# A zero-padded operand of 128 rows for the second product of the RWKV scan step

## The chip, the cores and the metric

The kernel runs on one core of one Trainium2 chip. The metric is the device time of one execution in microseconds (us), as the median of several runs. The profile shows one execution, taken by the hardware profiler. Its engines are PE (the matrix engine; PEld is its weight load), DVE (VectorE), ACT (ScalarE), POOL (GpSimd) and SP (SyncE, whose queue issues the transfers). L676 is line 676 of the kernel; in the changed kernel the lines behind line 614 stand one to two lines lower (the product of L664 is then at L665; L676 and what follows it keep their numbers).

## The reference

Two layers of a latent diffusion backbone over 1024 latent tokens and 256 context tokens of width 1024, in float32. Each layer projects its normed input into four groups of heads, mixes each group in its own way (2-D neighbourhood attention, multi-head latent attention, RWKV-7 time mixing in both directions, differential attention), joins them in an output projection, and then runs a gated channel mixer. The change lies in the RWKV group, a recurrence with a state of 64x64 per head:

```
def rwkv7_scan(r, decay, k, v, a, b, s0, reverse):
    def step(S, inp):
        r_t, w_t, k_t, v_t, a_t, b_t = inp
        sa = jnp.einsum('bhij,bhj->bhi', S, a_t)
        S = S * w_t[:, :, None, :] + sa[..., None] * b_t[:, :, None, :] + v_t[..., None] * k_t[:, :, None, :]
        return S, jnp.einsum('bhij,bhj->bhi', S, r_t)
    ...
    s_final, y = lax.scan(step, s0, xs, reverse=reverse)
```

There are four heads and two directions.

## The kernel before

The recurrence is done in chunks of 64 tokens. Ahead of the scan, `prep_gen` and `lanes_gen` make for each chunk the small matrices that a step needs and keep them in device memory; the scan loads them as `SG` (slices `ARM`, `RB`, `BT`) and `XB` (the inverse of a triangular 64x64 matrix per head and direction).

`rw_step_gen` is the scan: 20 steps of 64 tokens per layer, 40 in all. A step works on two directions `d`, two head pairs `p` and the two heads `e` of a pair; head `e` sits in rows 64e to 64e+63. All its sums go to one tile of the matrix engine's memory, `pall`. A step is a chain:

1. L664: eight products of 128 rows give `pd`. L667: ACT copies all of `pd` to `Dt`.
2. L676: eight products of `XB` with `Dt`, each on the 64 rows of its head, give `psa`. L678 and L679: ACT copies the half of head 0, and DVE the half of head 1, into `V1`, whose other halves hold the chunk's values. (In the trace `V1` is called V.)
3. L688: eight products of 128 rows with `V1` give `pss`. L696: DVE adds them to the decayed state and writes the next state into `VS`.
4. L706 and L708: sixteen products give the output `py`, which L712 (ACT) copies to `yt`, and L716 stores.

The scan is one of several generators that are advanced in turns: the attention of two groups runs beside it, and the modulation of the next part (`ada_gen`, tiles `adw` and `adaps`), later `rw_out_gen`. `rw_out_gen` turns the scan's outputs into the RWKV part of the mixed rows: a chain of small products (L748, L757, L768, L774, L781) with DVE, ACT and POOL work between them, and at the end the store L784 of `oy` into `ymix`. A unit of it covers 256 tokens of one head pair, and starts when the scan has come far enough. When all groups have stored their part of `ymix`, the output projection loads it (L1775, tiles `h_l`), splits it and multiplies (tiles `pso`, at the helper's lines 140 to 142).

The kernel doesn't write out the order of an engine by hand. A scheduler with a model of its own simulates the program as it is built, and sets each engine's order from that. Each engine then runs its list in order, and so does SP with the transfers: whatever stands behind an instruction that waits, waits too. Where two instructions write one tile, the later one in the program waits for the earlier: L679 waits for L678, although their halves of `V1` are apart.

Of the kernel before, what the change touches and what calls it, by code (L numbers as in the profile page):

```python
# [9 lines left out]
F32 = mybir.dt.float32  # L10
F32R = mybir.dt.float32r
AF = mybir.ActivationFunctionType
# [5 lines left out]
P = 128  # L18
# [22 lines left out]
class K:  # L41
# [561 lines left out]
    def rw_step_gen(self, l, pool, sgp, yp, psp, ptag, need_ctx, F):  # L603
        nc = self.nc
        TT, ACT, MM = nc.vector.tensor_tensor, nc.scalar.activation, nc.tensor.matmul
        segs = ([8, 9] + list(range(8)), [9, 8] + list(range(8))[::-1])
        sg = {}

        def need(i):
            return max(self.SLOT.index(segs[d][i]) for d in range(2))  # L610

        def step_y(i):
            return i >= 2 or need_ctx

        SZ = pool.tile([P, 2, 2, 2, 64], F32, name="SZ", bufs=1)
        for e in range(2):
            nc.gpsimd.memset(SZ[64 - 64 * e:128 - 64 * e, e], 0.0)

        def seg(i):
            SG = sgp.tile([P, 2, 1792], F32, tag="SG", name="SG", bufs=2)  # L620
            XB = pool.tile([P, 2, 4, 64], F32, tag="XB", name="XB", bufs=2)
            VS = pool.tile([P, 2, 2, 2, 2, 64], F32, tag="VS", name="VS", bufs=2)
            W = pool.tile([P, 2, 2, 2], F32, tag="W", name="W", bufs=2)
            for d in range(2):
                sl = self.SLOT.index(segs[d][i])
                vt = self.rvt[sl, d].rearrange("(c s) e p i -> e s c (p i)", c=2)
                for e in range(2):
                    q = slice(64 - 64 * e, 128 - 64 * e)
                    nc.sync.dma_start(VS[q, :, e, d].rearrange("s c p i -> s c (p i)"), vt[e])
                nc.sync.dma_start(SG[:, d], self.rsg[sl, d])  # L630
                nc.sync.dma_start(XB[:, d].rearrange("p u t -> p (u t)"), self.rxf[sl, d].rearrange("p u c t -> p (u c t)"))
                nc.gpsimd.tensor_copy(W[:, :, d], self.Wc[:, sl, d].rearrange("p (a c) -> p c a", a=2))
            if i == 0:
                for e in range(2):
                    nc.gpsimd.memset(VS[64 * e:64 * e + 64, 0, e], 0.0)
            BT = SG[:, :, 0:512].rearrange("p d (e u t) -> p d e u t", e=2, u=4)
            RB = SG[:, :, 512:768].rearrange("p d (u t) -> p d u t", u=4)
            ARM = SG[:, :, 768:1792].rearrange("p d (e u t) -> p d e u t", e=2, u=4)
            sg[i] = (XB, RB, BT, ARM, W, VS)

        while F["lanes"] <= need(0):
            yield
        seg(0)
        for _ in range(3):
            yield
        for step in range(20):
            i, c = step // 2, step % 2
            if c == 1 and i + 1 < 10:
                while F["lanes"] <= need(i + 1):
                    yield  # L650
            if c == 0 and i + 1 < 10 and F["lanes"] > need(i + 1):
                seg(i + 1)
            XB, RB, BT, ARM, W, VS = sg[i]
            V1 = pool.tile([P, 2, 2, 2, 64], F32, tag="V1", name="V1", bufs=2)
            pall = psp.tile([P, 2, 2, 2, 64], F32, tag=ptag, name="pall")
            pd, psa = pall[:, 0], pall[:, 1]
            tmp = pool.tile([P, 2, 2, 64], F32, tag="stmp", name="stmp", bufs=1)
            for e in range(2):
                q = slice(64 - 64 * e, 128 - 64 * e)
                nc.gpsimd.tensor_copy(V1[q, e], VS[q, c, e])  # L660
            for d in range(2):
                for p in range(2):
                    for e in range(2):
                        MM(pd[64 * e:64 * e + 64, d, p], ARM[:, d, e, 2 * p + c, 0:64], VS[:, c, e, d, p], start=True, stop=True)  # L664
            yield  # L665
            Dt = pool.tile([P, 2, 2, 64], F32, tag="Dt", name="Dt", bufs=2)
            ACT(Dt, pd, AF.Copy)  # L667
            for e in range(2):
                r = slice(64 * e, 64 * e + 64)
                nc.gpsimd.tensor_tensor(out=tmp[r], in0=VS[r, c, e], in1=W[r, c, :, :, None].to_broadcast([64, 2, 2, 64]), op=ALU.mult)  # L670
            yield
            for d in range(2):
                for p in range(2):
                    for e in range(2):
                        r = slice(64 * e, 64 * e + 64)
                        MM(psa[r, d, p], XB[r, d, 2 * p + c], Dt[r, d, p], start=True, stop=True)  # L676
            yield
            ACT(V1[0:64, 0], psa[0:64], AF.Copy)  # L678
            nc.vector.tensor_copy(V1[64:128, 1], psa[64:128])  # L679
            if step_y(i):  # L680
                for e in range(2):
                    nc.gpsimd.tensor_copy(SZ[64 * e:64 * e + 64, e], V1[64 * e:64 * e + 64, e])
            yield
            pss, py = pall[:, 0], pall[:, 1]
            for d in range(2):
                for p in range(2):
                    for e in range(2):
                        MM(pss[64 * e:64 * e + 64, d, p], BT[:, d, e, 2 * p + c], V1[:, e, d, p], start=True, stop=True)  # L688
            yield
            if step < 19:  # L690
                if c == 1 and i + 1 not in sg:
                    seg(i + 1)
                nVS = sg[i + c][5]
                for e in range(2):
                    r = slice(64 * e, 64 * e + 64)
                    TT(out=nVS[r, 1 - c, e], in0=tmp[r], in1=pss[r], op=ALU.add)  # L696
            yield
            if not step_y(i):
                yield
                continue  # L700
            for d in range(2):
                for p in range(2):
                    u = 2 * p + c
                    r = [slice(64 * e, 64 * e + 64) for e in range(2)]
                    for e in range(2):
                        MM(py[r[e], d, p], VS[:, c, e, d, p], ARM[:, d, e, u, 64:P], start=True, stop=False)  # L706
                    for e in range(2):
                        MM(py[r[e], d, p], SZ[:, e, d, p], RB[:, d, u], start=False, stop=True)  # L708
            yield
            if c == 0:  # L710
                yt = yp.tile([P, 2, 2, P], F32, tag="yt", name="yt", bufs=2)
            ACT(yt[:, :, :, c * 64:c * 64 + 64], py, AF.Copy)  # L712
            if c == 1:
                for d in range(2):
                    s = segs[d][i]
                    nc.sync.dma_start(self.ryd[d, :, :, s * P:(s + 1) * P], yt[:, d])  # L716
                F["seg"] = i
# [1583 lines left out]
```

## Time and profile before

| | |
|---|---|
| median of 3 runs | 4310.83 us (4297.64 to 4321.85) |
| the profiled execution | 4318.05 us, its span 4316.3 us |
| mean granted clock of the matrix engine | 0.955 of full speed |
| busy share of the span | PE 93%, PEld 77%, DVE 66%, ACT 46%, POOL 19% |
| the two scans | from 627 to 930 us and from 2890 to 3173 us |

The span runs from the first to the last instruction. A busy matrix engine is not one at its peak. The clock is the share of full speed that the throttle granted.

### The profile page before, as it was taken

How to read it: one execution, taken by the hardware profiler on the slowest of the kernel's cores; microseconds unless marked ns; L12 is line 12 of the kernel's file. 1: busy time of each engine (PE TensorE's matmuls, PEld its weight loads, DVE VectorE, ACT ScalarE, POOL GpSimd, SP SyncE). 2: the span in 40 equal slices, each digit the busy share in tenths (PEclk: the TensorE clock that was granted, in tenths of full speed). 3: DMA queues.
4: the chain of work that ended last, by engine and by line, in shares of the span. 5: the costliest groups of instructions: out<-in, count | busy, mean ns of one | idle time of the engine just before them, and what ended most of it. 6: DMA issues, size and time to landing. Idle time of an engine off the chain costs nothing. (4 is left out here: it accounts for less than half of the span.)

```text
span 4316.3 us, 76712 instructions
## 1 busy us (share of the span) xinstructions
PE 4027.8 (93%) x29152; PEld 3319.9 (77%) x29152; DVE 2866.8 (66%) x5946; ACT 1982.7 (46%) x4386; POOL 801.9 (19%) x1320
## 2 busy tenths in 40 slices
PE   6999969999999999899998999969999999999998
PEld 4887856677777778788887887856677777788998
DVE  6577686656676765655556667686776766557666
ACT  4444435535554544433334444435545555435443
POOL 3244122212211112000001344122313111111000
PEclk7999979999999999999999999979999999999999
DMA  6444676655523243221213344687636332333332
GB/s 198 151 134 141 204 226 204 224 160 142 151 82 107 78 149 115 71 64 65 64 59 115 137 135 139 204 233 223 206 98 175 104 106 74 125 104 126 94 98 74
DMA packets 423199, 578.40 MB, mean 134 GB/s; under 512 B 109100, under 2 KB 287660, under 8 KB 421296
## 3 DMA queue, kind: packets, MB, share of 16 engines
q1 hardware_dynamic: 422832, 573.51, 42.9%
q8 instruction: 230, 3.77, 0.4%
q14 instruction: 137, 1.12, 0.1%
HBM read 433.47 MB, written 139.92 MB: 133 GB/s over the span
## 5 line engine op out<-in xcount | busy, mean ns | idle before, releaser
L141 PE MATMUL psm<-h_l,whi 128*128 128x512 f32 (+1 forms) x2112 | 710.3, 336 | 9.2 <-DVE h_l L258 9.0
L140 PE MATMUL psm<-h_h,whi 128*128 128x512 f32 (+1 forms) x2112 | 713.5, 338 | 2.3 <-ACT h_h L257 2.3
L142 PE MATMUL psm<-h_h,wlo 128*128 128x512 f32 (+1 forms) x2112 | 709.0, 336 | 0.0
L1888 DVE SCALAR_TENSOR_TENSOR x<-psm,mod,x 128x258 f32<-128x258 f32 (+2 forms) x616 | 327.0, 555 | 288.3 <-PE psm L142 287.9
L973 ACT ACTIVATE sm_P<-psL,sm_n 128x512 f32<-128x512 f32 (+1 forms) x672 | 392.8, 593 | 266.6 <-DVE sm_n L964 238.5
L141 PEld LDWEIGHTS psm<-h_l,whi 128*128 128x128 f32 x2112 | 399.4, 189 | 54.1 <-DVE h_l L258 12.0
L140 PEld LDWEIGHTS psm<-h_h,whi 128*128 128x128 f32 x2112 | 399.4, 189 | 52.0 <-DVE x L1888 4.0
L142 PEld LDWEIGHTS psm<-h_h,wlo 128*128 128x128 f32 x2112 | 399.1, 189 | 43.4 <-issue 0.2
L962 DVE TENSOR_REDUCE sm_m<-psL 128x1 f32<-128x512 f32 (+1 forms) x640 | 353.0, 578 | 88.0 <-PE psL L803 43.3
L140 PE MATMUL psm<-gh,dhi 128*128 128x510 f32 (+3 forms) x1056 | 364.8, 347 | 10.1 <-ACT mb L1852 5.1
L133 ACT ACTIVATE whi<-wst 128x1024 fp32r<-128x1024 f32 x176 | 186.6, 1060 | 401.2 <-PE psm L141 376.7
L141 PE MATMUL psm<-gl,dhi 128*128 128x510 f32 (+3 forms) x1056 | 357.7, 339 | 0.1
L142 PE MATMUL psm<-gh,dlo 128*128 128x510 f32 (+3 forms) x1056 | 357.4, 339 | 0.0
L134 DVE TENSOR_TENSOR wlo<-wst,whi 128x1024 fp32r<-128x1024 f32 x176 | 214.8, 1220 | 169.6 <-ACT whi L133 169.5
L1032 PE MATMUL psV<-PT,V 128*64 128x128 f32 x3488 | 299.3, 283 | 1.2 <-DVE sm_n L964 0.7
L1011 PE MATMUL psT<-ident,sm_P 128*128 128x128 f32 x1744 | 287.3, 287 | 10.6 <-DVE sm_P L1001 6.2
L1032 PEld LDWEIGHTS psV<-PT,V 128*64 128x64 f32 x3488 | 208.8, 137 | 83.7 <-issue 63.7
L1011 PEld LDWEIGHTS psT<-ident,sm_P 128*128 128x128 f32 x1744 | 206.4, 145 | 69.8 <-issue 29.7
L140 PEld LDWEIGHTS psm<-gh,dhi 128*128 128x128 f32 x1056 | 199.6, 189 | 44.6 <-ACT mb L1852 9.3
L142 PEld LDWEIGHTS psm<-gh,dlo 128*128 128x128 f32 x1056 | 200.2, 190 | 21.7
L141 PEld LDWEIGHTS psm<-gl,dhi 128*128 128x128 f32 x1056 | 200.4, 190 | 18.1 <-issue 0.7
L803 PE MATMUL psL<-K,Q 96*128 96x512 f32 (+1 forms) x400 | 148.8, 437 | 68.7 <-DMA Q<-dfq 34.4
(381 smaller groups left out, 9264.7 us busy)
## 6 DMA issues: line engine op xcount, KB each, us to landing
wst<-in_w_up_dram SPq DMA_DIRECT2D x176, 512.0 KB
wst<-in_w_down_dram SPq DMA_DIRECT2D x88, 512.0 KB
adw<-in_ada_w_dram SPq DMA_DIRECT2D x80, 512.0 KB
SG<-rsg SPq DMA_DIRECT2D x40, 896.0 KB
wst<-in_w_out_dram SPq DMA_DIRECT2D x96, 256.0 KB
rsg<-ARM SPq DMA_DIRECT2D x20, 1024.0 KB
K<-dfk SPq DMA_DIRECT2D x16, 960.0 KB
wst<-in_w_rw_dram SPq DMA_DIRECT2D x28, 512.0 KB
```

What stands on the lines that cost most here:

```text
L133: nc.scalar.activation(hi[:, :n], st[:, :n], AF.Copy)
L134: nc.vector.tensor_tensor(out=lo[:, :n], in0=st[:, :n], in1=hi[:, :n].bitcast(F32), op=ALU.subtract)
L140: mm(out, ah, bh, start=first, stop=False)
L141: mm(out, ah, bl, start=False, stop=False)
L142: mm(out, al, bh, start=False, stop=last)
L803: nc.tensor.matmul(ps, ld[0][0:96, j], ld[1][j // 2][0:96, j % 2, o:o + n], start=True, stop=True)
L962: nc.vector.tensor_reduce(out=m[:, j, i:i + 1], in_=src, axis=AX.X, op=ALU.max)
L973: ACT(Pt[:, off:off + n], s["L"][j][t][:, to:to + n], AF.Exp, bias=neg, accum_out=sm[:, j, i:i + 1])
L1011: nc.tensor.transpose(pt[:, j], Ph[:, (bb + j) * P:(bb + j + 1) * P], self.ident)
L1032: nc.tensor.matmul(s["po"][64 * h:64 * h + 64, 0], V[:, kts[i], h], s["PT"][h][:, i], start=i == 0, stop=i == nk - 1, tile_position=(0, 64 ...
L1888: STT(out=x[:, s:e], in0=ps[:, s:e], scalar=mod[:, v, 40 + m:41 + m], in1=x[:, s:e], op0=ALU.mult, op1=ALU.add)
```

## The change

The copy of `pd` is cut in two, as that of `psa` is already: ACT copies the rows of head 0, DVE those of head 1. They go into the two planes of a tile `DZ` whose other halves are set to zero once per layer (two more memsets on POOL each time). With that, the eight products of L676 take all 128 rows of `XB`: the rows of the other head meet zeros. `Dt` had two buffers, `DZ` has one of the same size in all.

```
-        SZ = pool.tile([P, 2, 2, 2, 64], F32, name="SZ", bufs=1)
-        for e in range(2):
-            nc.gpsimd.memset(SZ[64 - 64 * e:128 - 64 * e, e], 0.0)
+        DZ, SZ = (pool.tile([P, 2, 2, 2, 64], F32, name=n, bufs=1) for n in ("DZ", "SZ"))
+        for t in (DZ, SZ):
+            for e in range(2):
+                nc.gpsimd.memset(t[64 - 64 * e:128 - 64 * e, e], 0.0)
...
-            Dt = pool.tile([P, 2, 2, 64], F32, tag="Dt", name="Dt", bufs=2)
-            ACT(Dt, pd, AF.Copy)
+            ACT(DZ[0:64, 0], pd[0:64], AF.Copy)
+            nc.vector.tensor_copy(DZ[64:128, 1], pd[64:128])
...
                     for e in range(2):
-                        r = slice(64 * e, 64 * e + 64)
-                        MM(psa[r, d, p], XB[r, d, 2 * p + c], Dt[r, d, p], start=True, stop=True)
+                        MM(psa[64 * e:64 * e + 64, d, p], XB[:, d, 2 * p + c], DZ[:, e, d, p], start=True, stop=True)
```

The scheduler sets the order anew. The lists of the two kernels are the same up to the first scan step, differ from there to the output projection of each layer, and are the same again elsewhere. Three places show how. On the matrix engine, the second step of the first scan stood so before (L1011, L1032, L803 and L1038 are attention, L1556 the modulation):

```order
L664 MATMUL pall<-VS,SG 64x64 x8
L1011 MATMUL psT<-ident,sm_P 128x128 x4
L1032 MATMUL psV<-PT,V 64x128
L1556 MATMUL adaps<-adw,sc_60 32x256 x4
L1032 MATMUL psV<-PT,V 64x128
L803 MATMUL psL<-K,Q 128x512
L1032 MATMUL psV<-PT,V 64x128
L803 MATMUL psL<-K,Q 128x256
L803 MATMUL psL<-K,Q 128x512
L676 MATMUL pall<-Dt,XB 64x64 x8
L1011 MATMUL psT<-ident,sm_P 128x128 x6
```

Now:

```order
L665 MATMUL pall<-VS,SG 64x64 x8
L1556 MATMUL adaps<-adw,sc_60 32x256 x4
L803 MATMUL psL<-K,Q 128x512
L803 MATMUL psL<-K,Q 128x256
L1038 MATMUL psV<-ident,o_ss 64x128 x2
L803 MATMUL psL<-K,Q 128x512
L676 MATMUL pall<-DZ,XB 64x64 x8
L803 MATMUL psL<-K,Q 128x512
L1032 MATMUL psV<-PT,V 64x128
```

Other work fills the time in which `Dt` or `DZ` is written, and it is chosen anew. Over all 40 steps the mean count of products between the first and the second product of a step goes from 11.9 to 17.3, and the scan falls behind the rest of the list: its last step stands 254 products later in the first layer and 134 in the second.

At the end of the second layer's scan stage, the matrix engine's list from the last product of `rw_out_gen` (L781) was this before (L873 is attention too):

```order
L781 MATMUL opg<-og,rwup 128x256
L873 MATMUL psL<-K,Q 128x128 x2
L873 MATMUL psL<-K,Q 128x256 x2
L873 MATMUL psL<-K,Q 128x512 x2
L1011 MATMUL psT<-ident,sm_P 128x128 x3
L1032 MATMUL psV<-PT,V 64x128 x5
```

and 39 more rows stood between these and the next attention (L803), beside which the output projection begins. Now:

```order
L781 MATMUL opg<-og,rwup 128x256
L1011 MATMUL psT<-ident,sm_P 128x128 x2
L1032 MATMUL psV<-PT,V 64x128 x3
L1038 MATMUL psV<-ident,rec 64x128 x2
L1011 MATMUL psT<-ident,sm_P 128x128 x6
L1032 MATMUL psV<-PT,V 64x128 x12
L1038 MATMUL psV<-ident,rec 64x128 x2
L140 MATMUL pso<-h_h_35190,wohi 128x512
```

The last unit of `rw_out_gen` has moved to the end of the stage. In the first layer it stands there too, closer still: its L774 is the row right ahead of the output projection.

The list of SP at the same place in the second layer: before (x and K, Q, V are loads for what follows; h_l is the load for the output projection):

```order
L784 DMA ymix<-oy 128x256
L2035 DMA x_2_35167<-xd 128x512
L2035 DMA x_3_35168<-xd 128x512
L2035 DMA x_4_35169<-xd 128x512
L850 DMA nb<-in_rpbp_dram 128x2x512
L2028 DMA cw<-in_conv_dram 128x88
L2035 DMA x_5_35170<-xd 128x512
L2035 DMA x_6_35171<-xd 128x512
L2035 DMA x_7_35172<-xd 128x512
L885 DMA lv<-in_lamb_dram 128x128
L888 DMA sub<-in_subln_dram 128x1
L796 DMA K<-dfk 96x2560 x2
```

with three loads of Q, one of V and a store of attention (L1068) behind them, and then h_l. Now:

```order
L784 DMA ymix<-oy 128x256
L2035 DMA x_2_35173<-xd 128x512
L2035 DMA x_3_35174<-xd 128x512
L2035 DMA x_4_35175<-xd 128x512
L2035 DMA x_5_35176<-xd 128x512
L2028 DMA cw<-in_conv_dram 128x88
L2035 DMA x_6_35177<-xd 128x512
L2035 DMA x_7_35178<-xd 128x512
L885 DMA lv<-in_lamb_dram 128x128
L888 DMA sub<-in_subln_dram 128x1
L1775 DMA h_l_35191<-ymix 128x512
L1068 DMA ymix<-ot 128x512
```

The loads of K, Q and V now stand behind those of h_l, and the last store of `rw_out_gen` still stands ahead of the loads that it was ahead of.

## Rows read from the trace of the kernel before

**Rows 1.** Windows of both scans: length, busy us (instructions) PE/PEld/DVE/ACT/POOL, clock, DMA share, GB/s.
```profile
627.00:930.00 303.00, 271.36 (x3495) 198.11 (x3495) 194.88 (x476) 143.16 (x424) 81.86 (x169) 0.91 0.69 209
2890.00:3173.00 283.00, 261.08 (x3410) 196.31 (x3411) 196.51 (x480) 145.86 (x436) 80.19 (x164) 0.97 0.67 197
```

**Rows 2.** The matrix engine's waits in the first scan: total us, times, longest.
```profile
PE adaps L1556 <- DMA adw<-in_ada_w_dram: 11.8, 3, 6.4
PE psL L803 <- DMA Q<-dfq: 7.9, 1, 7.9
```

**Rows 3.** Tile pall: durations (ns, min/median/max); then what its instructions' engines waited for (us, times).
```profile
L664 PEld LDWEIGHTS pall<-VS,SG x640: 132/138/232, 627.1 to 3162.3; 128*64 128x64 f32 x160
...
L667 ACT ACTIVATE Dt<-pall x40: 380/383/408, 629.4 to 3163.6; 128x256 f32<-128x256 f32 x40
...
L679 DVE COPY V<-pall x40: 427/428/429, 631.4 to 3167.7; 64x256 f32<-64x256 f32 x40
...
  DVE V L679: 16.7, 24
...
  ACT Dt L667: 5.4, 10
```

**Rows 4.** Timeline of ACT and DVE: the first and the last of 40 pairs.
```profile
631.03 0.38 ACT L678 ACTIVATE V<-pall 64x256 f32<-64x256 f32 x1 [1.22 <-PE pall L676]
631.45 0.43 DVE L679 COPY V<-pall 64x256 f32<-64x256 f32 x1 [0.30 <-ACT V L678]
...
3167.26 0.38 ACT L678 ACTIVATE V<-pall 64x256 f32<-64x256 f32 x1 [0.38 <-PE pall L676]
3167.66 0.43 DVE L679 COPY V<-pall 64x256 f32<-64x256 f32 x1 [0.29 <-ACT V L678]
```

**Rows 5.** Timeline of the matrix engine: start, duration, line, then rows*columns used.
```profile
2905.07 1.09 PE L1032 MATMUL psV<-PT,V 128*64 128x128 f32 x16
2906.09 0.68 PE L676 MATMUL pall<-Dt,XB 64*64 64x64 f32 x16
2906.70 0.65 PE L1032 MATMUL psV<-PT,V 128*64 128x128 f32 x6
...
3037.49 0.64 PE L664 MATMUL pall<-VS,SG 128*64 128x64 f32 x16
3037.96 0.83 PE L1032 MATMUL psV<-PT,V 128*64 128x128 f32 x12
```

**Rows 6.** Timeline of SP at the end of the second layer's scan stage.
```profile
3324.31 0.32 SPq L784 DMA_DIRECT2D ymix<-oy  x1
3324.67 1.40 SPq L2035 DMA_DIRECT2D x<-xd  x3
...
3327.22 0.61 SPq L2028 DMA_DIRECT2D cw<-in_conv_dram  x1
3327.88 2.33 SPq L2035 DMA_DIRECT2D x<-xd  x3
3330.25 0.43 SPq L885 DMA_DIRECT2D lv<-in_lamb_dram  x1
...
3343.86 1.57 SPq L1775 DMA_DIRECT2D h_l<-ymix  x1
```

**Rows 7.** Timeline of the matrix engine there: last L781, next attention, output projection.
```profile
3323.06 0.70 PE L781 MATMUL opg<-og,rwup 64*128 64x256 f32 x2
...
3348.74 0.86 PE L803 MATMUL psL<-K,Q 96*128 96x512 f32 x3
...
3351.16 0.49 PE L140 MATMUL pso<-h_h,wohi 128*128 128x512 f32 x1 [1.57 <-ACT h_h L1776]
```

**Rows 8.** Timeline of the matrix engine in the first layer: the last unit of rw_out_gen begins.
```profile
1101.12 0.59 PE L748 MATMUL opm<-oy,bones 128*128 128x256 f32 x2
```

**Rows 9.** Timeline of SP in the first layer: last store of rw_out_gen, first load of h_l.
```profile
1117.57 0.33 SPq L784 DMA_DIRECT2D ymix<-oy  x1
...
1143.58 1.10 SPq L1775 DMA_DIRECT2D h_l<-ymix  x1
```

## The prediction

> **What bounds the kernel now.** I began with the engines' busy time in the two stretches in which the scan runs [rows 1]. The matrix engine works 271 of 303 us in the first and 261 of 283 in the second; DVE, the next, works 195 and 197. So the scan runs in the shade of the attention beside it: the matrix engine sets the pace and has 32 + 22 = 54 us of idle time in all. Next I asked what it waits for there. The largest waits are for transfers: 11.8 us for the modulation's weights and 7.9 us for one load of queries [rows 2]. The waits of the scan's own products came third: over both layers, the engines of the tile `pall` waited 16.7 us in 24 places for the DVE copy of `psa`, and 5.4 us in 10 places for the ACT copy of `pd` [rows 3]. Last I read how the stage ends: in the second layer the last store of `rw_out_gen` is issued at 3324.31 us and the first load for the output projection at 3343.86, so the scan's followers have 19.6 us to spare [rows 6]; in the first layer it is 1143.58 - 1117.57 = 26.0 us [rows 9]. A later scan costs nothing until that is used up.
>
> **The products (-1 us).** The block of L676 is 16 records (8 products, each in two passes). Is it dearer or cheaper on 128 rows? The block of L664 has the same count and columns on 128 rows. What a block takes is the time from its start to that of the next one: 2906.70 - 2906.09 = 0.61 us for L676 and 3037.96 - 3037.49 = 0.47 us for L664, each followed by an L1032 block [rows 5]. The 0.14 us is no matter of rows as such: L676 (64 by 64) is followed by another shape there and L664 (128 by 64) by its own. So the change saves about 0.14 us wherever L676 stands next to a block of 128 by 64. In the order before, 13 of the 40 blocks have such a block ahead of them and 8 behind: at most 21 x 0.14 = 2.9 us. The new order as a whole has 1458 changes of shape against 1450, which gives 1.1 us back. I take -1; the ends are -11 (if all 80 edges were saved) and +1.
>
> The Trainium skill, "TensorEngine Tiling (Array Packing)", Key Properties, says that changing the tiling mode drains the engine; the 0.14 us agrees, and says that this is small. A rule of the Trainium skill, "TensorE: Matmul & The Clock Gate", Part 3, speaks against the change: weight loads overlap running products only where the row groups differ, and on 128 rows they no longer do. Loads that stand bare would cost 16 of them per block at 138 ns [rows 3]: 40 x 16 x 0.138 = 88 us more, a time of about 4399. The L664 block, already on 128 rows, takes 0.47 us for 16 records, so its loads do not stand bare; I give that outcome 1 in 100.
>
> **The copies (0 us).** ACT's copy goes from 128 to 64 rows of the same 256 elements; L678, the same half copy, takes 0.38 us [rows 4], as the whole copy does (383 ns [rows 3]). Nothing is saved. DVE gets 40 copies more of 0.428 us [rows 3], 17.1 us. Cover: DVE is idle 303 - 195 + 283 - 197 = 194 us of the two stretches. Without that cover it costs up to +17; I take 0. The four memsets more on POOL come ahead of the scan, on an engine that works 82 of 303 us [rows 1]: 0.
>
> **The wait of L676 (+6 us).** The two copies of `DZ` write one tile, so DVE's waits for ACT's, as L679 does for L678. L676 then waits for the pair. The first and the last pair take 631.88 - 631.03 = 0.85 and 0.83 us [rows 4]; the mean of the 40 is 1.49, since DVE often has other work ahead. Today's single copy takes 0.38. So each step gets about 1.1 us longer: 40 x 1.1 = 44 us, if the scan set the pace. It doesn't; the matrix engine has other work, and the new order puts 17.3 instead of 11.9 products there. The nearest row is the wait for the pair `V1`: 16.7 us in place of 5.4, +11.3 [rows 3]. Some of these are waits of weight loads under running products, so I take half, +6. The ends are 0 and +11; queued behind the waiting L676 is the attention, and behind the DVE copy the softmax.
>
> **The end of the stage (+10 us).** A scan that is 20 times 1.1 us later per layer eats the 26.0 and 19.6 us of spare time, and the order shows that: the last L781 stands just ahead of the output projection.
> Second layer. The work behind L781 is 8 products of L1011, 15 of L1032 (two records each; 16 records take 1.02 us [rows 5]) and 4 small ones: about 1 + 1.9 + 0.5 = 3.4 us. Today this attention ends at 3348.74 [rows 7], so L781 starts at about 3345.3. Its store is issued 3324.31 - 3323.06 = 1.25 us later [rows 6, 7], at 3346.6. Behind the store in SP's list stand six loads of x (1.40 + 2.33), `cw` (0.61) and two small ones (0.43 each, the second like the first [rows 6]): 5.2 us. The first load of `h_l` goes out at 3351.8 instead of 3343.86, +8, and nothing covers it, because K and Q of the next attention are now loaded behind it. Ends: 0, if the last unit comes as early as today, and +12, if its chain is slower than the simulated order.
> First layer. Here seven of the eight loads of `h_l` are ahead of that store, but L774 stands right ahead of the output projection on the matrix engine. Today the last unit takes 1117.57 - 1101.12 = 16.5 us from L748 to its store [rows 8, 9], with other work between its parts. In the new order about 3 us of products lie between L748 and L774. The projection waits for its split rows anyhow, 1.6 us in the second layer [rows 7]. I take +2, between 0 and +13 (16.5 less 3).
>
> **The sum.** -1 + 0 + 6 + 8 + 2 = +15 us. The profiled execution took 4318.05 us around a span of 4316.3, so the same execution would take 4333. It lay 7.2 above the median of the runs, 4310.83; so I predict 4326, +0.35%. A measurement of this kernel can tell about 0.5% (21.6 us) from no change, and this is below.
>
> **The rivals.**
> Slower: the late last unit of `rw_out_gen` holds up both layers. Place: L784 in SP's list and L774 on the matrix engine. For it speak the order, and that the unit is a chain over five engines that the simulation takes to be short; against it, that today's unit is stretched by the work between. Price: +12 and +13 at the ends of their ranges, with +6 of the scan's wait and -1: +30, 4341. It decides once the two ends together pass 21.6 - 5 = 17 us.
> No cost at all: real steps aren't longer, since the matrix engine has its other work, and the last unit comes in time. Then -1 to +3: about 4312. For it: only 5.4 + 16.7 of 54 us idle come from these waits. Against it: the order itself puts the unit late, and an engine runs its list in order.
> Faster: the shifted scan moves the waits for transfers. The matrix engine now does attention where it waited for the modulation's weights and the queries, 11.8 + 7.9 = 19.7 us [rows 2], and the clock, 0.91 there [rows 1], keeps up. With -1 to -5 from the shapes and nothing lost at the ends: -23, 4288. Against it: nothing in the change makes these loads earlier.
>
> **Chances.** Forecast 0.45, no cost 0.14, slower rival 0.34, faster rival 0.06, bare loads 0.01. The forecast and the second rival lie within 0.5%: 0.59. Slower by more: 0.35. Faster: 0.06. The forecast's own range is 4315 to 4335. Eight times in ten: below, down to 4303, the no-cost rival with the spread of the runs (up to 13 us below their median) is in; above, 4352 takes in the slower rival with 11 us of the DVE copies uncovered.
>
> **What would show it.** Right: a block of L676 next to L1032 takes 0.47 us; L676 waits for DVE in about 24 places, some 17 us; the pair of `DZ` copies takes 1.5 us in the mean; DVE's busy time is up by 17 us; the second layer's first `h_l` load is issued some 5 us behind the last L784, and the matrix engine idles about 8 us more ahead of the output projection. Wrong: the last L784 with more than 10 us to the first `h_l` load (then the ends cost nothing), a matrix engine's idle time in the scans that is above 65 us (then the scan sets the pace) or below 40 (then the transfers were hidden).

## The result and the profile after

The changed kernel takes 4339.96 us (median of 7 runs, 4328.58 to 4351.23) against 4310.83: the ratio is 1.0072, with a 95% interval of 1.0053 to 1.0091, so it is 31 us slower (23 to 39). Its profiled execution took 4338.15 us around a span of 4336.3. An execution of either kernel lies up to some 13 us beside its median, so that a single pair of profiles can't place a few us.

The two windows of [rows 1], of the changed kernel:

```profile
627.00:930.00 303.00, 278.29 (x3560) 203.55 (x3560) 211.67 (x526) 150.12 (x447) 73.58 (x164) 0.95 0.72 214
2890.00:3173.00 283.00, 261.32 (x3231) 197.49 (x3229) 196.57 (x488) 144.15 (x429) 73.68 (x152) 0.94 0.64 190
```

The matrix engine is a little fuller than before (25 and 22 us idle, before 32 and 22). But these windows no longer hold the whole scan: its last L712 starts at 960.56 instead of 937.29, and 3198.84 instead of 3172.04.

The tile `pall`, to set against [rows 3]; the rows behind the dots give what its instructions' engines waited for (us, times):

```profile
L676 PEld LDWEIGHTS pall<-DZ,XB x640: 132/138/231, 635.0 to 3193.0; 128*64 128x64 f32 x160
...
L667 ACT ACTIVATE DZ<-pall x40: 364/377/381, 628.2 to 3190.1; 64x256 f32<-64x256 f32 x40
L668 DVE COPY DZ<-pall x40: 427/428/428, 628.6 to 3190.5; 64x256 f32<-64x256 f32 x40
...
  DVE DZ L668: 10.1, 19
  DVE V L679: 8.6, 16
```

The waits of the matrix engine (its products and its weight loads together) for the last copy of a pair are 10.1 us at L676 and 8.6 at L688, 18.7 in all, less than the 5.4 + 16.7 = 22.1 before. At L676 alone they rose, from 5.4 to 10.1. By these rows the longer step costs nothing.

The first and the last pair of `DZ` copies on ACT and DVE, as [rows 4] for `V`:

```profile
628.16 0.38 ACT L667 ACTIVATE DZ<-pall 64x256 f32<-64x256 f32 x1 [5.86 <-PE pall L665]
628.57 0.43 DVE L668 COPY DZ<-pall 64x256 f32<-64x256 f32 x1 [0.41 <-ACT DZ L667]
...
3190.06 0.38 ACT L667 ACTIVATE DZ<-pall 64x256 f32<-64x256 f32 x1 [0.73 <-PE pall L665]
3190.47 0.43 DVE L668 COPY DZ<-pall 64x256 f32<-64x256 f32 x1
```

A pair takes 0.84 us at the least. The mean of the 40, from the start of L667 to the end of L668, is 1.58 us; the copy that it replaces took 0.39.

A block of L676 between two of L1032, as in [rows 5], and one between two of L1011:

```profile
3111.49 0.66 PE L1032 MATMUL psV<-PT,V 128*64 128x128 f32 x8
3111.98 0.64 PE L676 MATMUL pall<-DZ,XB 128*64 128x64 f32 x16
3112.44 0.60 PE L1032 MATMUL psV<-PT,V 128*64 128x128 f32 x6
...
2949.18 0.69 PE L676 MATMUL pall<-DZ,XB 128*64 128x64 f32 x16 [0.15 <-DVE DZ L668]
2949.80 0.66 PE L1011 MATMUL psT<-ident,sm_P 128*128 128x128 f32 x4
```

The first takes 0.46 us to the next block, where the block on 64 rows took 0.61; the second takes 0.62. Of the 40 blocks, 28 run at the full clock, with no other product among theirs and no wait behind them: two have products of 128 by 64 on both sides (0.46 us), six only behind (0.52), three only ahead (0.57), and the other 17 take 0.62. On 64 rows a block takes 0.61 whatever stands beside it.

SP at the end of the second layer's scan stage, as [rows 6]:

```profile
3349.91 0.32 SPq L784 DMA_DIRECT2D ymix<-oy  x1
3350.28 1.87 SPq L2035 DMA_DIRECT2D x<-xd  x4
...
3356.50 3.56 SPq L1775 DMA_DIRECT2D h_l<-ymix  x7
3360.10 1.33 SPq L796 DMA_DIRECT2D K<-dfk  x2
3361.51 0.61 SPq L799 DMA_DIRECT2D Q<-dfq  x1
```

The matrix engine there, as [rows 7]:

```profile
3348.66 0.70 PE L781 MATMUL opg<-og,rwup 64*128 64x256 f32 x2
...
3359.55 0.80 PE L140 MATMUL pso<-h_h,wohi 128*128 128x512 f32 x1 [5.95 <-ACT h_h L1776]
...
3375.13 1.19 PE L803 MATMUL psL<-K,Q 96*128 96x512 f32 x2 [6.75 <-DMA Q<-dfq]
```

The last store is 25.6 us later than before. The output projection waits 5.95 us for its split rows, and the next attention 6.75 us for a load of Q that now stands behind `h_l`. In the first layer the projection waits 5.43 us, in its first round, for the last of its eight rows, where it waited 1.49 before at its start:

```profile
1138.36 0.80 PE L140 MATMUL pso<-h_h,wohi 128*128 128x512 f32 x1 [5.43 <-ACT h_h L1776]
```

The windows from the first scan step to the last work of an engine, before and after, one row of each:

```profile
627.16:4312.02 3684.86, 3496.80 (x25648) 2885.46 (x25648) 2428.18 (x5130) 1703.87 (x3812) 610.33 (x1037) 0.97 0.41 127
```

```profile
625.80:4332.21 3706.41, 3499.44 (x25648) 2883.14 (x25648) 2445.76 (x5169) 1703.78 (x3812) 619.04 (x1038) 0.96 0.41 126
```

The matrix engine is busy 2.6 us longer and idle 18.9 us longer (207.0 against 188.1), at the same mean clock of the whole execution (0.955 and 0.957). So in the sum the loss is waiting. It is not spread evenly. From the first scan step of a layer to the end of its output projection, the first layer and then the second, before:

```profile
627.16:1736.60 1109.44, 1062.54 (x8218) 820.91 (x8218) 735.60 (x1674) 553.12 (x1363) 216.17 (x353) 0.97 0.47 142
2890.69:3916.70 1026.01, 982.30 (x7668) 769.57 (x7669) 693.10 (x1526) 520.10 (x1258) 195.75 (x323) 0.98 0.45 136
```

and now:

```profile
625.80:1732.30 1106.50, 1057.27 (x8218) 814.77 (x8218) 744.40 (x1692) 552.33 (x1363) 219.71 (x352) 0.97 0.47 143
2882.64:3937.30 1054.66, 998.44 (x7669) 781.60 (x7669) 704.76 (x1546) 520.78 (x1259) 196.64 (x323) 0.96 0.44 132
```

In these two executions the first layer loses nothing, and the second 28.7 us: 12.5 of idle time, and 16.1 of busy time, with the same products at a lower mean clock (0.98, now 0.96). The question is what this comes from.

### The profile page after: what moved, and what is told of

The parts are those of the page before. It is cut to its first block, busy times and chain, and to the rows that moved or that the text cites. A ratio compares the mean times of both kernels' runs of the same rounds, so it can differ in the third digit from the quotient of the medians.

```text
span 4336.3 us, 76725 instructions
## 1 busy us (share of the span) xinstructions
PE 4029.6 (93%) x29152; PEld 3315.7 (76%) x29152; DVE 2886.1 (67%) x5986; ACT 1982.2 (46%) x4386; POOL 816.6 (19%) x1324
## 5 line engine op out<-in xcount | busy, mean ns | idle before, releaser
L1032 PE MATMUL psV<-PT,V 128*64 128x128 f32 x3488 | 304.0, 286 | 1.9 <-DVE ot L1065 1.0
L1011 PE MATMUL psT<-ident,sm_P 128*128 128x128 f32 x1744 | 289.5, 287 | 10.1 <-DVE sm_P L1001 4.7
L1032 PEld LDWEIGHTS psV<-PT,V 128*64 128x64 f32 x3488 | 210.3, 138 | 89.1 <-issue 67.9
L1011 PEld LDWEIGHTS psT<-ident,sm_P 128*128 128x128 f32 x1744 | 205.1, 145 | 68.7 <-issue 28.2
L1021 ACT ACTIVATE PT<-psT 128x512 f32<-128x512 f32 (+2 forms) x300 | 151.8, 525 | 140.5 <-PE psT L1011 139.0
L141 PEld LDWEIGHTS psm<-gl,dhi 128*128 128x128 f32 x1056 | 200.0, 189 | 18.7 <-DVE gl L1871 0.9
```

What stands on the lines that cost most here:

```text
L141: mm(out, ah, bl, start=False, stop=False)
L1011: nc.tensor.transpose(pt[:, j], Ph[:, (bb + j) * P:(bb + j + 1) * P], self.ident)
L1021: ACT(dst, src, AF.Copy)
L1032: nc.tensor.matmul(s["po"][64 * h:64 * h + 64, 0], V[:, kts[i], h], s["PT"][h][:, i], start=i == 0, stop=i == nk - 1, tile_position=(0, 64 ...
```

## The experiments

Theory 1: the late end of the scan stage costs the time (waits for `h_h` and for K and Q). Theory 2: the longer step costs it, wherever the end stands. Theory 3: the products of 128 rows cost it. The times measured are medians; what a run takes over before is its ratio to runs of the kernel before on the same chip, less 1, times 4311 us. A dict `prio` in the scheduler moves a generator's instructions forward (positive) or back, and nothing else in the program; several runs use it to set the scan's place in the order.

**Split copy, products on 64 rows** (in the kernel before)

```
-            ACT(Dt, pd, AF.Copy)
+            ACT(Dt[0:64], pd[0:64], AF.Copy)
+            nc.vector.tensor_copy(Dt[64:128], pd[64:128])
```

> The copy of pd is split between ACT and DVE as in the change, but into Dt (two buffers), and L676 stays on 64 rows. The matrix engine's order equals the changed kernel's up to the middle of the second scan, and the end of both layers' stages is in the same order. Theory 1 (the late end of the scan stage costs the time, above all in the second layer): 20 to 30 us over before, the same as the changed kernel within 8 us, L676 taking 0.61 us beside an L1032 block again. Theory 2 (the copies and the longer step cost it): the same 20 to 30. Theory 3 (the products of 128 rows cost it): within 8 us of before. So this run tells theory 3 from the other two.

Measured: 4337.59 us, ratio 1.0062 (1.0045 to 1.0079), 27 us over before, as the changed kernel. Theory 3 falls: the rows cost nothing that can be told. Nor do they save: the gain at the borders is at most the few us that the intervals leave.

**Old step, late scan** (in the kernel before)

```
-    prio = {}
+    prio = {"scan": -1000}
```

> The kernel before with its old step (one ACT copy, 64 rows), but the scan's instructions get a lower priority in the scheduler, so that its last step stands about as late in the list as in the changed kernel (5215 and 17031 products from the start; changed kernel 5242 and 17030; before 4988 and 16892). The end of the second layer's stage stands in the same order as in the changed kernel: 28 products from the last L781 to the output projection, ten transfers from the last L784 to h_l, K and Q behind h_l. Theory 1 (late end): 18 to 30 us over before, most of it between 3310 and 3440 us, with a wait of 5 to 8 us for Q ahead of L803. Theory 2 (the step's own cost): within 5 us of before. Theory 3 (products): within 5 us.

Measured: 4314.10 us, ratio 1.0010 (0.9997 to 1.0023). Theory 1 missed. Its waits are there all the same: the matrix engine's waits by what ended them (us in total, times, longest), over the whole execution, before:

```profile
PE psL L803 <- DMA Q<-dfq: 34.4, 3, 13.5
...
PE adaps L1556 <- DMA adw<-in_ada_w_dram: 16.8, 6, 6.4
...
PE pso L140 <- ACT h_h L1776: 3.1, 2, 1.6
```

and in this run:

```profile
PE psL L803 <- DMA Q<-dfq: 42.1, 4, 13.8
...
PE pso L140 <- ACT h_h L1776: 12.3, 4, 6.3
...
PE adaps L1556 <- DMA adw<-in_ada_w_dram: 2.3, 2, 1.9
```

The changed kernel waits 11.4 us for `h_h` and 36.5 for Q. The modulation's weights, 16.8 us before, cost 2.3 here, so a gain may hide the price of the end. This run alone doesn't settle theory 1.

**New step, scan ahead**, and **new step, only the first layer ahead** (in the changed kernel)

```
-    prio = {}
+    prio = {"scan": 20}
```

and, in the second run, `{"scan": 10}`.

> The changed kernel with its new step, but the scan gets a slightly higher priority (20) in the scheduler. The last step stands at 5103 and 16899 products (changed 5242 and 17030, before 4988 and 16892). The end of the second layer's stage is in the order of before (169 products from the last L781 to the output projection, K and Q ahead of h_l); that of the first layer is between the two (24 products, K and Q behind h_l). Theory 1: 0 to 10 us over before, nothing lost at the second layer's end. Theory 2: 20 to 30 us over before, as the changed kernel. Theory 3: 20 to 30.

> As the run with priority 20, with 10 instead. Its first layer ends in the same order as that run's (last step at 5103, 24 products), its second as the changed kernel's (last step at 17030, 28 products, K and Q behind h_l). The difference between these two runs is the price of the second layer's end. Theory 1: 15 to 25 us above the run with priority 20. Theories 2 and 3: within 6 us of it.

Measured: 4335.54 us, ratio 1.0052 (1.0034 to 1.0070), and 4337.21 us, 1.0063 (1.0042 to 1.0083): 22 and 27 us over before. The second layer's end is that of before in the one and that of the changed kernel in the other, and their medians are 1.7 us apart. Theory 2 expected both.

**New step, both ends early, and the control** (in the changed kernel and in the kernel before)

```
-    prio = {}
+    prio = {"scan": 20, "ada": -50}
```

> The changed kernel's new step, with priorities in the scheduler (scan 20 up, modulation 50 down) under which both layers end as in the kernel before: K, Q and V are loaded ahead of h_l in both, and 79 and 104 products lie between the last L781 and the output projection (before 188 and 169, changed 1 and 28). Theory 1, now in two parts (the late ends give waits for h_h and Q of some 13 to 16 us; the runs so far showed them also in the old step with a late scan, where the waits for the modulation's weights, 16.8 us, had gone): 0 to 10 us over before, the waits for h_h and Q together at most 3 us above before's. Theory 2 (the step itself costs, wherever the end stands): 20 to 30 us over before.

> The kernel before with the priorities of the run with both ends early (scan 20 up, modulation 50 down); a control for the priorities. Its second layer ends in the same way as that run's (104 products), its first as before's (188). All theories: within 8 us of before; what the run with both ends early takes above this one is the price of the new step when the ends cost nothing: 0 to 10 by theory 1, 20 to 30 by theory 2.

Measured: new step 4334.85 us, ratio 1.0051 (1.0035 to 1.0067), 22 us over before; old step 4309.70 us, 1.0002 (0.9991 to 1.0013). Under the same priorities the new step costs 25 us between the medians, though K, Q and V are loaded ahead of `h_l` in both layers of both kernels. But the run didn't bring what theory 1 asked of it, waits for `h_h` and Q at most 3 us above before's: they come to 62.7 us, against 37.5 before and 54.0 in the control. Behind the scans alone they are 3.1 us before, 12.1 in the control, 20.6 here, 21.1 in the changed kernel and 27.3 in the old step with a late scan, which is 4 us over before. So the early order of the loads does not take the waits away; yet by these profiles at most 9 of the 25 us can come from them, and over the runs the loss does not follow them. Theory 1 falls as the main cause. The windows of the new step and the control from the first scan step to the last work of an engine, the new step's first:

```profile
629.53:4331.41 3701.88, 3501.06 (x25657) 2881.94 (x25657) 2451.72 (x5177) 1710.65 (x3822) 617.69 (x1038) 0.97 0.42 126
```

```profile
628.49:4305.35 3676.86, 3502.22 (x25657) 2885.03 (x25657) 2429.96 (x5137) 1709.00 (x3821) 602.62 (x1036) 0.97 0.42 127
```

The matrix engine is equally busy, and idle 200.8 against 174.6 us. Of the 25 us between these windows, 10 lie between the first layer's projection and the second scan (1158.6 against 1148.7 us), where no scan step runs; that stretch takes 1148.7 to 1158.6 us over all the profiles. So this pair of executions shows the size of the loss, but not its place. The rest of the runs ask which part of the new step does this.

**Both half copies of `DZ` by ACT** (in the changed kernel)

```
-            nc.vector.tensor_copy(DZ[64:128, 1], pd[64:128])
+            ACT(DZ[64:128, 1], pd[64:128], AF.Copy)
```

> The products of 128 rows and the padded tile stay, but ACT makes both half copies, one behind the other: no copy is added to VectorE, and the wait ahead of L676 gets 0.4 us longer instead of 1.1. Both layers end in the same way as in the run with both ends early (79 and 104 products). Theory 1: 0 to 10 us over before. Theory 2 in the form that VectorE's 40 copies cost: 0 to 5 over before, and so 15 to 25 under the run with both ends early. Theory 2 in the form that the longer wait of the step costs: 5 to 12 over before.

Measured: 4322.39 us, ratio 1.0022 (1.0010 to 1.0034), 9.5 us over before: what the longer wait was to cost.

**VectorE's time alone** (in the kernel before)

```
             ACT(Dt, pd, AF.Copy)
+            dd = pool.tile([P, 2, 2, 64], F32, tag="dd", name="dd", bufs=1)
+            for e in range(2):
+                nc.vector.tensor_copy(dd[64:128], VS[64:128, c, e])
```

> The kernel before, its step unchanged, with two copies more on VectorE in each step (64 by 256 elements from VS to a tile that nobody reads; some 0.2 to 0.45 us each, 40 steps). No wait of the step is added. The first layer ends in the order of before, the second still earlier (277 products from the last L781 to the output projection). Theory 2 in the form that VectorE's time costs: 10 to 25 us over before. Theory 1 and the form with the longer wait: within 6 us of before.

Measured: 4313.07 us, ratio 1.0012 (0.9998 to 1.0025). The 80 copies took 0.29 us each, 23 us, more than the 17 us of the changed kernel; they cost 5 us (-1 to 11). VectorE's time is not the main part, though a few us of it can't be told from none.

**The other pair, `V1`, by ACT alone** (in the kernel before)

```
-            nc.vector.tensor_copy(V1[64:128, 1], psa[64:128])
+            ACT(V1[64:128, 1], psa[64:128], AF.Copy)
```

> The kernel before with the other pair of half copies (L678, L679 into V1) made by ACT alone, one behind the other, instead of ACT and VectorE. By the runs so far such a pair takes 0.78 us on ACT and 1.5 on ACT and VectorE together, so the step's chain gets 40 x 0.7 = 28 us shorter. Theory 2 in the form that the length of the step's chain costs (so far 0.6 of each us that the chain gets longer): 10 to 18 us faster than before. Rival (the matrix engine is nearly full in the kernel before, so a shorter chain finds nothing to save; only a longer one costs): within 6 us of before.

Measured: 4298.62 us against 4314.27, ratio 0.9966 (0.9947 to 0.9985): 15 us faster than before, as the chain form said. It is the fastest of all kernels here. The first pair, on ACT's timeline:

```profile
636.00 0.38 ACT L678 ACTIVATE V<-pall 64x256 f32<-64x256 f32 x1 [1.22 <-PE pall L676]
636.40 0.38 ACT L679 ACTIVATE V<-pall 64x256 f32<-64x256 f32 x1
```

One engine does in 0.78 us what the two do in 1.49 in the mean [rows 4]: the second copy stands right behind the first, and no work of another engine's list lies between them. The order of the second layer's end has moved here too, to 277 products between the last L781 and the projection; it is the same as in the run with VectorE's time alone, which gained nothing.

**Three ACT copies in a row** (in the kernel before)

```
             ACT(Dt, pd, AF.Copy)
+            ACT(dd, Dt, AF.Copy)
+            ACT(Dt, dd, AF.Copy)
```

> The old step on 64 rows, but pd goes through three ACT copies in a row (pd to Dt, Dt to a second tile, and back) instead of one: the chain gets some 0.75 us longer, about as much as from the start of L664 to L676 was added in the changed kernel (0.84 us), with no copy on VectorE. The ends of both layers stand late in the order, later than in the changed kernel (one product from the last L781 to the output projection). Chain form: 18 to 35 us over before. Form in which VectorE's part in the chain costs: at most 12 us over before, as when ACT made both half copies (9.5).

Measured: 4332.65 us, ratio 1.0048 (1.0029 to 1.0067), 21 us over before, with no copy on VectorE. The first of the 40 on ACT's timeline:

```profile
629.98 0.38 ACT L667 ACTIVATE Dt<-pall 128x256 f32<-128x256 f32 x1 [5.89 <-PE pall L664]
630.40 0.42 ACT L669 ACTIVATE dd<-Dt 128x256 f32<-128x256 f32 x1
630.84 0.42 ACT L670 ACTIVATE Dt<-dd 128x256 f32<-128x256 f32 x1
```

In the mean the three copies took 1.57 us longer than the one of before, not the expected 0.75. Length without VectorE brings a loss of this size; but the ends stand latest here, which may be a part of it.

**`Dt` by VectorE** (in the kernel before)

```
-            ACT(Dt, pd, AF.Copy)
+            nc.vector.tensor_copy(Dt, pd)
```

> The old step on 64 rows, with the one copy of pd to Dt made by VectorE (0.43 us) instead of ACT (0.38 us): the chain gets longer only by what the copy waits behind VectorE's other work. Chain form: from the start of L664 to L676 some 3.5 us instead of 3.16, so 40 x 0.35 x 0.6 = 8 us over before, 3 to 14. Form in which VectorE's part in the chain costs: 18 to 30 over before.

Measured: 4314.30 us, ratio 1.0009 (0.9991 to 1.0028), 4 us over before (-4 to 12): VectorE in the chain is not dear in itself.

**Changed kernel with `V1` by ACT** (the edit of the fastest run, in the changed kernel)

> The changed kernel with both half copies of V1 made by ACT, as in the run that was 15 us faster than before: the pair of DZ lengthens the chain, the pair of V1 shortens it. If the length of the step's chain is what costs, the two add up: 29 - 15 = 14 us over before (6 to 20), and the time from the start of L664 to L688 is about 7.3 us (before 6.8, changed 8.0). Rival (VectorE's copy of DZ costs in itself, by holding up the softmax or the matrix engine's order): 20 to 30 over before, as the changed kernel.

Measured: 4327.57 us, ratio 1.0026 (1.0008 to 1.0044), 11 us over before. The two edits add up about as the chain form said, and L664 to L688 takes 7.23 us, where 7.3 was expected.

All runs together. "Copies" is the mean over the 40 steps of the time from the start of the first copy to the end of the last, worked out from the timelines of ACT and DVE, for `Dt` or `DZ` and for `V1`:

| kernel | Dt or DZ | V1 | sum, us | over before, us (95%) |
|---|---|---|---|---|
| V1 by ACT | 0.39 | 0.78 | 1.17 | -15 (-23 to -6) |
| Dt by VectorE | 0.42 | 1.42 | 1.84 | 4 (-4 to 12) |
| old step, control | 0.39 | 1.45 | 1.84 | 1 (-4 to 6) |
| VectorE's time alone | 0.39 | 1.47 | 1.86 | 5 (-1 to 11) |
| before | 0.39 | 1.49 | 1.88 | 0 |
| old step, late scan | 0.39 | 1.51 | 1.90 | 4 (-1 to 10) |
| changed, V1 by ACT | 1.23 | 0.78 | 2.01 | 11 (3 to 19) |
| DZ by ACT | 0.78 | 1.39 | 2.17 | 9 (4 to 15) |
| split, 64 rows | 1.51 | 1.27 | 2.78 | 27 (19 to 34) |
| new step, first layer ahead | 1.45 | 1.36 | 2.81 | 27 (18 to 36) |
| new step, both early | 1.50 | 1.32 | 2.82 | 22 (15 to 29) |
| new step, scan ahead | 1.44 | 1.39 | 2.83 | 22 (15 to 30) |
| changed | 1.58 | 1.40 | 2.98 | 31 (23 to 39) |
| three ACT copies | 1.96 | 1.52 | 3.48 | 21 (13 to 29) |

But for the last row, the loss follows the length of the copies, whichever engine makes them and wherever the ends stand. Four kernels have the same order of transfers at the second layer's end, K, Q and V ahead of `h_l`: the control, the changed kernel with `V1` by ACT, `DZ` by ACT, and the new step with both ends early. Their copies take 1.84, 2.01, 2.17 and 2.82 us, and they lie 1, 11, 9 and 22 us over before. The closest pairs give the rate: V1 by ACT, 15 us for 40 x 0.71 = 28; new step against its control, 25 for 40 x 0.98 = 39; changed kernel, 31 for 40 x 1.10 = 44. That is 0.5 to 0.7 us per us of chain; the longest chain gives less, 21 for 64. In each of the three pairs one VectorE copy a step comes or goes with the length, so a few us of VectorE's time may be in the rate. `DZ` by ACT has no such copy more than before: 9.5 us for 40 x 0.39 = 16, which is 0.6.

The whole step follows less well. From the start of L664 to that of L688 it takes 6.78 us before, 7.96 in the changed kernel and 7.68 with both ends early, but 7.46 in the control, which loses nothing. So it is the length of the copies that the runs show as the cause, and not yet the way from there to the time.

## Why the prediction was wrong where it was

The time lies in the wide range, but above the forecast's own (4315 to 4335) and on the slower rival's side: 31 us, not 15. That it lies in the wide range is luck in part, since this reached so far up for a rival whose cause did not hold. Of the signs that were named, two failed: L676 waits for VectorE in 19 places, 10.1 us, not in 24 with 17, and the idle time ahead of the second output projection grows by 4.4 us (1.57 to 5.95), not by 8. Point by point:

**What bounds the kernel: half right.** The matrix engine does set the pace, and its idle time in the two windows even falls, from 54 to 46 us. But "the scan runs in the shade" was too strong: a chain 28 us shorter gave 15 us back, from the same kernel.

**The products (-1): not refuted.** The saving of 0.14 us came only where products of 128 by 64 stand on both sides (0.61 to 0.46); next to one such block it is 0.10 or 0.05, and elsewhere nothing. Over the 28 blocks that can be read this makes about 1 us, as forecast. The run on 64 rows shows no gain or loss of the products that a measurement can tell. That run also speaks against the bare weight loads (88 us), as the rows of 138 ns under blocks of 0.46 us do.

**The copies (0): right within 11 us**, by the run with VectorE's time alone.

**The wait of L676 (+6): this step failed.** I sized the longer step by the waits that the matrix engine has right at the tile, and set aside the 44 us as the case in which the scan sets the pace. At L676 they rose by 4.7 us, close to the +6, but at L688 they fell by 8.1, and the step still cost 22 to 25 us with both ends early. The price is 0.5 to 0.7 of the 44 us, and it doesn't show at the tile. The scheduler fills a longer step with other work; that the time is lost later, at other instructions, is what is left, and no run shows where. In the changed kernel's profile it is in the second layer. A rule of the Trainium skill, "Perfetto Trace Analysis", Optimization Strategy, says to look for the gaps on the engine that is being optimized and for what blocks it there. In this trace such gaps gave no price: those at the step's own tile went from 22.1 to 18.7 us while the kernel lost 31.

**The end of the stage (+10): seen, but not the cause it was taken for.** In the second layer the last L784 and `h_l` stand as forecast, 4.7 us apart, at 3354.57 instead of 3351.8. The projection begins 8.4 us later than before, as the +8 said, but that is luck: this execution came to the second scan 8.1 us earlier (2882.64 against 2890.69), and from there the projection begins 16.4 us later. The 6.75 us for Q was not in the sum. In the first layer the wait for the last of the rows is 5.43 us, where +2 was forecast, and the layer as a whole takes no longer. The slower rival named this end as its whole price, 12 + 13 us. The order with both ends early takes back 9 of the 31 us by the two ratios, and their intervals overlap. So, as far as the runs show, the rival had the time and not the cause.

**The statement that L679 waits for L678 because they write one tile** is not shown. Both copies also read one tile, `pall`, and no kernel here has the two halves in two tiles, so the runs can't tell the two reasons apart.

**What stays open.** Why a us of chain costs half a us, and through which waits in each order, isn't settled: each kernel has its own order, and the profiles of single executions differ by more than the terms. The late end was never priced alone, since the old step with a late scan also lost its waits for the modulation's weights, and the order with both ends early kept the waits of the ends.

## What to carry to other kernels

Price a longer dependency chain by its length times its count, not by the waits seen at its own instructions: where a scheduler fills the gaps, those waits may move little, and here 0.5 to 0.7 of the added length came back as time, for up to 44 us of it. Compare the same stretch of work in two profiles before naming a place: start times alone made one end look as forecast here. Two half copies on two engines weren't faster here than both on one (0.83 us at the least against 0.76): the second waits for the first anyway, and then for its own engine's list. Before taking a late end as the cause, move the end alone and, in another run, keep it and change the step.

## What was not expected of the hardware

In the wait of 5.95 us the granted clock drops to its lower level, and stays there behind it. Windows of the changed kernel at the second layer's end: ahead of the wait, in it, behind it and later (the granted clock is the third figure from the end):

```profile
3350.00:3353.50 3.50, 3.35 (x42) 2.61 (x38) 1.38 (x4) 2.19 (x5) 0.00 (x0) 1.00 0.70 207
3353.60:3359.50 5.90, 0.00 (x1) 0.00 (x0) 1.41 (x7) 1.06 (x3) 0.00 (x0) 0.87 1.01 319
3359.55:3363.30 3.75, 3.62 (x6) 1.91 (x7) 2.06 (x4) 1.88 (x3) 0.00 (x0) 0.50 0.94 304
3364.60:3368.00 3.40, 3.40 (x16) 2.69 (x14) 2.19 (x4) 1.34 (x3) 0.00 (x0) 0.97 1.05 249
```

In the third window it is 0.50, the level of 1.2 GHz, and a product of `pso` takes 0.63 to 0.80 us instead of 0.40. The kernel before pays for this too, although its wait at the same place is 1.57 us: there the engine works on for 1.74 us at the full level, and then the clock is 0.50 for 3.4 us.

```profile
3351.16:3352.90 1.74, 1.51 (x5) 1.02 (x6) 1.74 (x3) 1.74 (x4) 0.00 (x0) 1.00 0.98 331
3352.92:3356.30 3.38, 3.38 (x9) 2.64 (x8) 3.38 (x7) 2.66 (x5) 0.00 (x0) 0.50 0.74 261
```

The first twelve products of `pso` take 4.74 us before and 5.86 in the changed kernel, where twelve at the full level take 2.8. So the drop behind this wait adds about 1 us to the difference. Behind the wait of 6.75 us for Q, which the kernel before does not have, the clock is 0.50 again, and 6.05 us of work run at that level:

```profile
3375.13:3381.80 6.67, 6.05 (x14) 4.13 (x15) 2.89 (x6) 3.16 (x8) 0.00 (x0) 0.50 1.00 243
```

At the full level that work would take about half, by the products' 0.63 and 0.40 us and their starts 0.43 and 0.23 us apart. The two drops together are an estimated 4 us that the sum did not have.
